# The beginning of the second attention in another issue order on four engines, and its later part left to the scheduler

## The chip, the cores and the metric

The kernel runs on one core of a Trainium2 chip. A core has five engines that work side by side, each with its own instruction stream: PE (matrix products, written to the PSUM memory), DVE (vector work), ACT (scalar functions), POOL (more vector work, masks) and SP (issues transfers). POOL issues transfers too. Engines wait for each other through semaphores. An engine takes its instructions in the order in which they were issued to it, so an instruction that waits holds up all that stands behind it on the same engine.

The metric is the device time of one execution in microseconds (us), the median over several runs.

## The reference

The reference is one layer of a decoder trunk on 1024 tokens of width 1024. One input projection feeds four groups of heads; their gated outputs are put side by side, go through one output projection, are added to the input, and are normalised at the end:

```python
def forgetting_attention(q, k, v, log_f):        # the "second attention" here: fox
    cum = jnp.cumsum(log_f, axis=-1)
    ...
        logits = (jnp.einsum('bhqd,bhkd->bhqk', qb, k) * scale
                  + cb[..., None] - cum[:, :, None, :])
        logits = jnp.where(key_pos[None, :] <= q_pos[:, None], logits, -jnp.inf)
        return jnp.einsum('bhqk,bhkd->bhqd', jax.nn.softmax(logits, axis=-1), v)
...
def reference(x, norm_g, w_in, ..., w_out, final_g):
        h = rms_norm(x, norm_g[l])
        p = h @ w_in[l]
        y_fox = forgetting_attention(...)
        y_sb = stick_breaking_attention(...)     # the first attention here: sb
        y_rw = rwkv7_time_mix(...)
        y_lru = rg_lru(...)
        y = jnp.concatenate([
            y_fox * jax.nn.silu(fg.astype(f32)),
            y_sb * jax.nn.silu(sg.astype(f32)),
            y_rw * jax.nn.silu(rg.astype(f32)),
            y_lru * jax.nn.silu(lg.astype(f32)),
        ], axis=-1).astype(x.dtype)
        x = x + y @ w_out[l]
    return rms_norm(x, final_g)
```

## The kernel before

Most products are made of two or three products of rounded parts (a high and a low part of each factor), so that nearly every tile has a twin: `woh` and `wol` are the high and low parts of a block of the output weights, `PH` and `PL` those of transposed attention weights.

The kernel's last third, from about 400 us on, is what the change touches. There the first attention (sb) ends, the second (fox) runs, and PE has "fill" beside both. The fill beside sb is the input projections (`pj_fv`: the values of fox, the last of them). The fill beside fox is the output projection `po` (768 of its 1024 input rows: groups sb, RWKV, LRU), eight blocks of 128 tokens by two halves of columns. The remaining 256 input rows, those of fox itself, are `pofx` at the end, and the final norm follows.

Attention works in units: a pair of heads (0 or 1), a group g of 256 queries, a head o of the pair. In `fox_weights` a unit makes scores on PE (`zfox`, L1174, in one of two PSUM banks "g"), adds the forget term to them and takes the maximum on DVE (`atfox`, L1213; `Fb` is the forget row spread over all partitions, `FM` a masked piece of it that POOL makes at L1197), takes the exponential on ACT (L1222), a reciprocal on DVE (`sm`, L1226), and scales on ACT (L1229). In `values` PE transposes the weights (`ptfox`, L1246, in one of two PSUM banks "c"), ACT and DVE copy them out as `PH` and `PL` (L1251, L1252), and PE multiplies them with the values `VS` (`avfox`, L1256). ACT and DVE add the two halves up (`ypfox`, L1260 and L1261), DVE multiplies with the gate `gt` (L1145), and the result is written to memory (`yx_d`, L1391) through `yyfox`. The sb attention goes through the same `values` (`ptsb`, `PHsb`, `PLsb`, `avsb`). Digits in a name are pair-head, query block or group, and part: `PLsb331` is head 3, group 3, part 1; `zfox050` is head 0, query block 5, part 0.

The transfers around it: SP's queue brings keys (`KSfox`, L1117, four loads of 256 KB for a pair), the forget rows (`Fb`, L1129, 512 KB each), queries (`Q`, L1108, 64 KB), values (`VS`, L1124), gates (`gt`, L1132, 512 KB); POOL's queue stores the projected values (`p_fv`, L1006), and loads the output projection's left factors (`yc`, L1403, two loads of 768 KB for 256 tokens), the residual (`xt`, L1409, 256 KB) and raw output weights (`wor`, L1331). A block `po` is closed by DVE's addition `ac` (L1353), which needs `xt`.

The order of each engine's instructions is written out as numbers. `ORDERS` (from L55) has a text for each engine; `in_order()` (L1474) chains the instructions named there, one behind the other, without a wait between them; instructions that are not named are placed by the framework's list scheduler. `order()` (L1263) chains PE's fill between the attention's products in any case.

Of the kernel before, what the change touches and what calls it, by code (L numbers as in the profile page):

```python
# [42 lines left out]
for _name, _w in (  # L43
# [163 lines left out]
    ),  # L207
}
# [1342 lines left out]
```

## Time and profile before

| | us |
|---|---|
| runs before: lowest, median, highest | 625.92, 629.45, 630.3 |
| the profiled execution's own time | 629.03 |
| its span, first to last instruction | 627.1 |
| PE busy in the span | 608.5 (97%) |
| DVE busy | 489.8 (78%) |
| ACT busy | 390.7 (62%) |
| POOL busy | 200.8 (32%) |

The time lies 1.93 us above the span. Busy time says how much of the span an engine had an instruction under way; with PE at 97% it is PE's few idle stretches, and those in which its clock is low, that can be won or lost. The views used are: the table of windows (busy time of each engine in a stretch of time, the number of its instructions in brackets, then the granted clock of PE, the busy share of the transfer engines, and GB/s); the list of waits (an engine and line, who released it, total, number of times, longest); and the timeline (start, duration, engine, line, operation, result and operands, the number of merged instructions, and in brackets the idle time before it and who ended that). In the timeline neighbouring instructions overlap a little, since each row's duration runs to the end of its pipeline.

### The profile page before, as it was taken

How to read it: one execution, taken by the hardware profiler on the slowest of the kernel's cores; microseconds unless marked ns; L12 is line 12 of the kernel's file. 1: busy time of each engine (PE TensorE's matmuls, PEld its weight loads, DVE VectorE, ACT ScalarE, POOL GpSimd, SP SyncE). 2: the span in 40 equal slices, each digit the busy share in tenths (PEclk: the TensorE clock that was granted, in tenths of full speed). 3: DMA queues.
4: the chain of work that ended last, by engine and by line, in shares of the span. 5: the costliest groups of instructions: out<-in, count | busy, mean ns of one | idle time of the engine just before them, and what ended most of it. 6: DMA issues, size and time to landing. Idle time of an engine off the chain costs nothing.

```text
span 627.1 us, 11831 instructions
## 1 busy us (share of the span) xinstructions
PE 608.5 (97%) x4060; PEld 494.9 (79%) x4060; DVE 489.8 (78%) x1131; ACT 390.7 (62%) x722; POOL 200.8 (32%) x328
## 2 busy tenths in 40 slices
PE   8999999999999999999999999999999999999993
PEld 6867777778876687777888888879997788888882
DVE  6598687998996796978866988888774776857687
ACT  6797948451013378797534776567764657766575
POOL 2231421313113675444343220400223222322175
PEclk9999999999999999999999999999999899999997
DMA  8873766527351336721998665355498867763225
GB/s 288 305 220 87 193 176 152 143 101 183 108 165 62 103 99 222 241 100 71 254 300 270 202 211 159 134 169 168 143 273 298 261 207 248 256 197 135 84 102 201
DMA packets 86403, 114.35 MB, mean 182 GB/s; under 512 B 38151, under 2 KB 57927, under 8 KB 86344
## 3 DMA queue, kind: packets, MB, share of 16 engines
q1 hardware_dynamic: 69112, 57.81, 31.0%
q0 software_dynamic: 16656, 55.23, 26.1%
q8 instruction: 32, 0.52, 0.3%
q10 hardware_dynamic: 576, 0.56, 0.3%
q14 instruction: 27, 0.22, 0.1%
HBM read 79.31 MB, written 33.21 MB: 179 GB/s over the span
## 4 chain that ended last, share of the span: by engine, by line
PE 65%; DVE 13%; ACT 7%; DMA 7%; issue 6%; POOL 2%; SPq 1%; DVEq 0%; ACTq 0%; POOLq 0%
PE po L1351 9%; PE pj_fk L402 4%; PE pofx L1351 4%; PE pj_sg L402 4%; PE pj_fq L402 3%; PE pj_sq L402 3%; PE pj_rg L402 3%; PE pj_fg L402 3%; PE zsb L1174 3%; PE avfox L1256 3%; PE pj_v L402 3%; PE zfox L1174 2%; PE avsb L1256 2%; PE ptfox L1246 2%; DMA xr<-in_xT_dram 2%
## 5 line engine op out<-in xcount | busy, mean ns | idle before, releaser
L1351 PE MATMUL po<-woh,yc 128*128 128x512 f32 x192 | 69.6, 412 | 0.0
L1190 DVE TENSOR_TENSOR_SCAN atsb<-kp,atsb 128x128 f32<-128x128 f32 (+7 forms) x32 | 43.4, 1362 | 5.1 <-ACT atsb L1188 4.9
L1351 PE MATMUL po<-wol,yc 128*128 128x512 f32 x96 | 39.8, 414 | 0.0
L1222 ACT ACTIVATE atfox<-atfox,nb 128x128 f32<-128x128 f32 (+7 forms) x32 | 24.6, 770 | 23.9 <-DVE nb L1219 12.7
L1351 PEld LDWEIGHTS po<-woh,yc 128*128 128x128 f32 x192 | 34.8, 192 | 2.9
L1187 ACT ACTIVATE kp<-zsb 128x512 f32<-128x512 f32 (+3 forms) x48 | 23.6, 491 | 17.5 <-PE zsb L1174 17.0
L1252 DVE TENSOR_TENSOR PLfox<-ptfox,PHfox 128x512 fp32r<-128x512 f32 (+1 forms) x40 | 25.4, 636 | 10.4 <-ACT PHfox L1251 9.8
L1252 DVE TENSOR_TENSOR PLsb<-ptsb,PHsb 128x512 fp32r<-128x512 f32 (+1 forms) x40 | 25.1, 630 | 8.3 <-ACT PHsb L1251 7.5
L1251 ACT ACTIVATE PHsb<-ptsb 128x512 fp32r<-128x512 f32 (+1 forms) x40 | 22.1, 555 | 10.8 <-PE avsb L1256 5.9
L1251 ACT ACTIVATE PHfox<-ptfox 128x512 fp32r<-128x512 f32 (+1 forms) x40 | 21.9, 548 | 11.1 <-PE avfox L1256 9.7
L1174 PE MATMUL zsb<-KSsb,Q 128*128 128x512 f32 (+3 forms) x96 | 28.6, 357 | 0.0
L1174 PE MATMUL zfox<-KSfox,Q 128*128 128x512 f32 (+3 forms) x96 | 25.6, 349 | 2.2 <-DVE mx L1213 2.2
L1229 ACT ACTIVATE atfox<-atfox,sm 128x128 f32<-128x128 f32 (+7 forms) x32 | 23.4, 767 | 0.7 <-DVE sm L1226 0.7
L1188 ACT ACTIVATE atsb<-zsb 128x512 f32<-128x512 f32 (+3 forms) x48 | 23.4, 488 | 0.0
L749 POOL TENSOR_TENSOR Hp<-UV,PC 64x128 f32<-64x128 f32 x32 | 16.6, 518 | 21.3 <-DVE UV L796 17.6
L1174 PEld LDWEIGHTS zfox<-KSfox,Q 128*128 128x128 f32 x96 | 17.8, 191 | 6.2 <-DVE mx L1213 2.6
L1246 PE MATMUL ptsb<-ident,atsb 128*128 128x128 f32 x144 | 22.2, 272 | 0.4 <-DVE PLsb L1252 0.4
L1381 POOL TENSOR_TENSOR ac<-ac,fg 128x512 f32<-128x512 f32 x16 | 20.7, 1324 | 5.6 <-ACT ot L1359 5.6
L1213 DVE CUSTOM_DVE_ANT_0 atfox<-zfox,Fb 128x512 f32<-128x512 f32 (+3 forms) x40 | 20.9, 524 | 2.0 <-PE zfox L1174 1.8
L1246 PEld LDWEIGHTS ptfox<-ident,atfox 128*128 128x128 f32 x144 | 18.2, 140 | 5.5
L1246 PE MATMUL ptfox<-ident,atfox 128*128 128x128 f32 x144 | 22.2, 272 | 0.0
L1256 PE MATMUL avsb<-PLsb,VS 128*128 128x256 f32 x80 | 20.1, 286 | 0.9 <-DVE PLsb L1252 0.7
(547 smaller groups left out, 2161.6 us busy)
## 6 DMA issues: line engine op xcount, KB each, us to landing
yc<-yx_d POOLq DMA_DIRECT2D x16, 768.0 KB, 6.9
xn<-in_x_dram SPq DMA_DIRECT2D x8, 512.0 KB, 5.3
Q<-p_sq SPq DMA_DIRECT2D x64, 64.0 KB, 3.4
Q<-p_fq SPq DMA_DIRECT2D x64, 64.0 KB, 3.6
xt<-in_x_dram POOLq DMA_DIRECT2D x16, 256.0 KB, 6.1
out_dram<-ac SPq DMA_DIRECT2D x15, 256.0 KB, 2.1
xr<-in_xT_dram SPq DMA_DIRECT2D x6, 512.0 KB, 9.0
wor<-in_w_out_dram SPq DMA_DIRECT2D x9, 256.0 KB, 3.8
```

What stands on the lines that cost most here:

```text
L402: mm = nc.tensor.matmul(out[0:ww.shape[-1]], ww, xx[hf][:, k], start=(k == 0 and xx is xh and ww is wh), stop=(k == KT - 1 and ww is wl))
L1174: ((hi - c) / 2400, nc.tensor.matmul(z[:, c - lo:hi - lo], q, k, start=j == 0, stop=j == len(ops) - 1))
L1187: nc.scalar.activation(kp[:, lo:hi], z[:, 0:hi - lo], AF.Sigmoid, scale=-0.125)
L1188: nc.scalar.activation(at[:, lo:hi], z[:, 0:hi - lo], AF.Sigmoid, scale=0.125)
L1190: nc.vector.tensor_tensor_scan(rv, kp[:, 0:n][:, ::-1], rv, 0.0, op0=ALU.mult, op1=ALU.add)
L1222: exp = nc.scalar.activation(At[qb][:, 0:n], At[qb][:, 0:n], AF.Exp, bias=nb[:, qb:qb + 1], scale=0.125, accum_out=sm_[:, 0, qb:qb + 1])
L1229: nc.scalar.activation(At[qb][:, 0:n], At[qb][:, 0:n], AF.Copy, scale=sm_[:, 1, qb:qb + 1])
L1246: T.append((P / 1200, nc.tensor.transpose(pt[:, col:col + P], At[qb][:, (2 * m + j) * P:(2 * m + j + 1) * P], ident)))
L1251: nc.scalar.activation(PH[:, 0:w], pt[:, 0:w], AF.Copy)
L1252: nc.vector.tensor_tensor(PL[:, 0:w], pt[:, 0:w], PH[:, 0:w], op=ALU.subtract)
L1256: V.append(((c1 - c0) / 2400, nc.tensor.matmul(av[:, q0:256], VS[:, 2 * m + j, :], pp[:, c0:c1], start=m == 0 and j == 0 and pi == 0, stop ...
L1351: mm = nc.tensor.matmul(po, y, w, start=i == 0, stop=i == len(ops) - 1)
```

## The change

Only `ORDERS` changes. In the text of DVE, ACT, POOL and SP some numbers from the beginning of fox on stand in another order, and behind that beginning all five texts are cut off: what follows is placed by the scheduler. The table is 34 lines shorter, so that a line number of the old kernel is 34 higher than the new one's for the same statement. Two of the changed lines, SP's:

```diff
-        "266 207 242-245 267 260 275 246-249 276 223 284 268-271 261 277 262 278-280 232 286-289 274 290-293 313 "
-        "283 314 322 241 323 295 272 296-301 281 302 331 250 304 273 282 305-311 285 315-318 324-327 294 336 337 "
...
+        "266 207 242-245 267 260 275 246-249 276 223 284 268-271 261 277 262 278-280 232 286-289 274 290 293 292 "
+        "291 314 313 322 283 323 295-298 241 299 272 281 302 300 301 304 305 307 306 331 308 311 309 310 250 273 "
+        "282 315-318 285 324-327 294"
```

The built programs have the same instructions. PE's order is the same in both, row for row, also behind the place where its text ends. On the other engines rows move at several places. Three are shown; a row has the line, the operation, result and operands with their buffer numbers, and the size.

First, SP's queue where fox's keys of pair 0 (`KSfox1` is the second such tile) and the forget row `Fb1` are loaded. Before:

```order
L1108 DMA Q_4411<-p_fq_2265 64x256 x4
L1117 DMA KSfox1_6559<-p_fk_2418 64x1024
L1129 DMA Fb1_5960<-F_d_129 128x1024
L1117 DMA KSfox1_6559<-p_fk_2418 64x1024 x2
L1391 DMA yx_d_128<-yysb12_5291 128x2x256
L1117 DMA KSfox1_6559<-p_fk_2418 64x1024
L1108 DMA Q_4411<-p_fq_2265 64x256
L1124 DMA VS_4410<-p_fv_2720 128x4x128
L1108 DMA Q_4411<-p_fq_2265 64x256 x6
L1124 DMA VS_4410<-p_fv_2720 128x4x128
```

The same place of SP's queue now:

```order
L1083 DMA KSfox1_6559<-p_fk_2418 64x1024 x3
L1095 DMA Fb1_5960<-F_d_129 128x1024
L1083 DMA KSfox1_6559<-p_fk_2418 64x1024
L1074 DMA Q_4411<-p_fq_2265 64x256 x4
L1357 DMA yx_d_128<-yysb12_5291 128x2x256
L1074 DMA Q_4411<-p_fq_2265 64x256
L1090 DMA VS_4410<-p_fv_2720 128x4x128 x2
```

Two loads of keys now stand ahead of `Fb1` that stood behind it, and the first load of values stands behind four more rows, with the second right behind it.

Second, DVE at the same time of the program, where the last unit of sb (`PLsb33..`) overlaps the first of fox. Before:

```order
L1342 TENSOR_TENSOR wol21_5630<-wor21_5494,woh21_5629 128x512
L1252 TENSOR_TENSOR PLsb330_5421<-ptsb330_5415,PHsb330_5420 128x512
L1252 TENSOR_TENSOR PLsb331_5434<-ptsb331_5428,PHsb331_5433 128x512
L1226 RECIPROCAL sm_00_5970<-sm_00_5970 128x2
L1213 ISA atfox10_6012,mx10_6009<-zfox100_6013,FM10_6005 128x128
```

DVE's same place now:

```order
L1218 TENSOR_TENSOR PLsb330_5421<-ptsb330_5415,PHsb330_5420 128x512
L1116 TENSOR_TENSOR yysb12_5291<-ypsb12_5143,yysb12_5291 128x256
L1179 ISA atfox10_6012,mx10_6009<-zfox100_6013,FM10_6005 128x128
L1179 ISA mx10_6009 128x1
L1308 TENSOR_TENSOR wol21_5630<-wor21_5494,woh21_5629 128x512
L1218 TENSOR_TENSOR PLsb331_5434<-ptsb331_5428,PHsb331_5433 128x512
L1192 RECIPROCAL sm_00_5970<-sm_00_5970 128x2
```

`atfox10`, which needs `FM10` and through it `Fb1`, has moved ahead of `PLsb331`; `wol21` has come between them.

Third, DVE some 20 us later, where the first block of the output projection is closed (`ac0`). Before:

```order
L1353 TENSOR_TENSOR ac0_5527<-po00_5540,xt00_5538 128x512
L1218 TENSOR_REDUCE nb11_6134<-mx11_6119 128x2
L1219 TENSOR_SCALAR nb11_6134<-nb11_6134 128x2
L1201 MEMSET mx12_6263 128x6
L1226 RECIPROCAL sm_11_6121<-sm_11_6121 128x2
L1213 ISA atfox04_6187,mx02_6184<-zfox040_6188,Fb0_5950 128x512
```

DVE's same place now:

```order
L1179 ISA atfox04_6187,mx02_6184<-zfox040_6188,Fb0_5950 128x512
L1179 ISA mx02_6184 128x1
L1192 RECIPROCAL sm_11_6121<-sm_11_6121 128x2
L1111 TENSOR_TENSOR ypfox00_5963<-ypfox00_5963,gt_4412 128x256
L1179 ISA atfox04_6187,mx02_6184<-zfox041_6192,FM02_6180 128x128
L1179 ISA mx02_6184 128x1
L1319 TENSOR_TENSOR ac0_5527<-po00_5540,xt00_5538 128x512
L1218 TENSOR_TENSOR PLfox010_6090<-ptfox010_6084,PHfox010_6089 128x512
```

`atfox04<-zfox040` no longer stands behind `ac0` and the reciprocal. On POOL the load of `xt00` has moved from behind the two loads `yc10` to ahead of them. The gate's product `ypsb13*gt`, behind which SP loads the next gate, has moved on DVE from ahead of `atfox12` to behind it.

Later, where ACT rounds the last blocks of output weights, three of these have moved ahead of the copies of one unit. Before:

```order
L1251 ACTIVATE PHfox132_6504<-ptfox132_6499 128x512
L1260 ACTIVATE ypfox03_6339<-avfox03_6379 64x256
L1251 ACTIVATE PHfox133_6516<-ptfox133_6512 128x384
L1341 ACTIVATE woh71_5655<-wor71_5653 128x512
L1341 ACTIVATE woh00_6533<-wor00_6531 128x512
L1260 ACTIVATE ypfox03_6339<-avfox13_6472 64x256
L1341 ACTIVATE woh10_6539<-wor10_6537 128x512
```

ACT's same place now:

```order
L1307 ACTIVATE woh71_5655<-wor71_5653 128x512
L1217 ACTIVATE PHfox132_6504<-ptfox132_6499 128x512
L1307 ACTIVATE woh00_6533<-wor00_6531 128x512
L1307 ACTIVATE woh10_6539<-wor10_6537 128x512
L1217 ACTIVATE PHfox133_6516<-ptfox133_6512 128x384
```

On DVE `wol71`, `wol00` and `wol10` have moved in the same way against `PLfox132`, `PLfox133` and `atfox37`. In the final norm ACT scales `ac2` and takes a root ahead of the squares `ot10`, `ot11`, where one of the two scalings stood between them.

55 rows, old and new, of the table ORDERS are left out of this document.

## The prediction

> **What bounds the kernel now.** I read the page's head and its busy times first, then the windows of 5 us, to find where PE is not busy, then the timeline there. A window's columns are PE, PE's weight loads, DVE, ACT and POOL busy, PE's granted clock, the share of the transfer engines, GB/s.
>
> ```profile
> span 627.1 us, 11831 instructions
> PE 608.5 (97%) x4060; PEld 494.9 (79%) x4060; DVE 489.8 (78%) x1131; ACT 390.7 (62%) x722; POOL 200.8 (32%) x328
> ...
> 460.00:465.00 5.00, 4.64 (x40) 4.40 (x39) 4.08 (x13) 4.20 (x9) 0.00 (x0) 1.00 1.03 301
> 485.00:490.00 5.00, 2.91 (x9) 2.55 (x10) 3.63 (x11) 4.00 (x10) 1.33 (x3) 0.69 0.73 226
> 490.00:495.00 5.00, 5.00 (x29) 4.19 (x28) 3.61 (x15) 3.12 (x7) 1.69 (x3) 0.96 0.87 271
> 530.00:535.00 5.00, 5.00 (x30) 4.26 (x30) 3.77 (x11) 5.00 (x9) 0.77 (x2) 1.00 0.55 163
> ```
>
> PE is busy 97% of the span. In the window from 530 it is busy all the time at clock 1.00; idle PE time shows between 460 and 465 (0.36 us) and from 485 to 490 (2.1 us), and only with the second is the granted clock low (0.69, then 0.96). So a wait costs time here only where it reaches PE, and then one for one, plus what the clock loses behind it.
>
> **The stall that the change removes.** The rows of PE, DVE, ACT and POOL around 485:
>
> ```profile
> 484.49 0.40 PE L1351 MATMUL po<-wol,yc 128*128 128x512 f32 x1
> 487.09 1.22 PE L1174 MATMUL zfox<-KSfox,Q 128*128 128x512 f32 x2 [2.20 <-DVE mx L1213]
> 490.53 0.40 PE L1174 MATMUL zfox<-KSfox,Q 128*128 128x256 f32 x2
> ...
> 483.83 0.69 DVE L1353 TENSOR_TENSOR ac<-po,xt 128x512 f32<-128x512 f32 x1 [3.16 <-DMA xt<-in_x_dram]
> 486.27 0.17 DVE L1226 RECIPROCAL sm<-sm 128x2 f32<-128x2 f32 x1 [1.47 <-ACT atfox L1222]
> 486.35 0.67 DVE L1213 CUSTOM_DVE_ANT_0 atfox<-zfox,Fb 128x512 f32<-128x512 f32 x1
> ...
> 471.66 1.70 POOL L1403 DMA_DIRECT2D yc<-yx_d  x2 [1.20 <-PE zfox L1174]
> 473.34 0.56 POOL L1409 DMA_DIRECT2D xt<-in_x_dram  x1
> ```
>
> At 487.09 `zfox050` needs a bank that `atfox04<-zfox040` (486.35) frees. That stood on DVE behind `ac0`, which waited 3.16 us for `xt00` (issued at 473.34, behind 1.5 MB of `yc10`), and behind the reciprocal, which waited another 1.47 us for ACT. Now `atfox04<-zfox040` stands ahead of both, and `xt00` is issued ahead of `yc10`. PE's 2.20 us go. How much the clock lost behind them follows from the work up to 490.53: six products of 512 columns and four of 256. At full clock they follow each other as here:
>
> ```profile
> 473.96 0.39 PE L1351 MATMUL po<-wol,yc 128*128 128x512 f32 x1
> 474.19 0.62 PE L1351 MATMUL po<-woh,yc 128*128 128x512 f32 x2
> 474.65 0.27 PE L1256 MATMUL avfox<-PHfox,VS 128*128 128x256 f32 x1
> 474.77 0.28 PE L1256 MATMUL avfox<-PLfox,VS 128*128 128x256 f32 x1
> ```
>
> 0.23 us apart for 512 columns, 0.12 for 256: 6 x 0.23 + 4 x 0.12 = 1.86 us, against 490.53 - 487.09 = 3.44 measured. So 1.6 us went to the clock. Removed: 2.2 + 1.6 = 3.8 us. The ends: 0 if the wait only changes its name (below), 3.8 if nothing comes in its place.
>
> The Trainium skill's page "TensorE: Matmul & The Clock Gate" (section "Why this matters for your kernels") says that PE falls back to half clock after an idle gap of more than about 3 us. This trace disagrees: 2.20 us of idle were enough for 0.69. By the page only 2.2 us would go here, while a new gap of 3 us would cost its 1.6 us of half clock as well; the sum below would then be 631.8 instead of 630.2. I go by the trace for both.
>
> **The stall that the change brings.** Where sb ends, DVE, POOL, PE and SP did this, and the transfers of `KSfox` took (view of one tile, issue to landing):
>
> ```profile
> 466.92 0.29 DVE L1213 CUSTOM_DVE_ANT_0 atfox<-zfox,FM 128x128 f32<-128x128 f32 x1 [1.50 <-POOL FM L1197]
> 467.14 0.69 DVE L1342 TENSOR_TENSOR wol<-wor,woh 128x512 fp32r<-128x512 f32 x1
> 467.74 0.69 DVE L1252 TENSOR_TENSOR PLsb<-ptsb,PHsb 128x512 fp32r<-128x512 f32 x1
> 466.49 0.76 POOL L1197 TENSOR_SCALAR_AFFINE_SELECT FM<-Fb 128x256 f32<-128x256 f32 x2 [9.18 <-DMA Fb<-F_d]
> ...
> 464.81 0.66 PE L1246 MATMUL ptsb<-ident,atsb 128*128 128x128 f32 x4 [0.36 <-DVE PLsb L1252]
> 466.71 0.49 PE L1246 MATMUL ptsb<-ident,atsb 128*128 128x128 f32 x3
> ...
> 453.54 0.33 SPq L1129 DMA_DIRECT2D Fb<-F_d  x1
> 453.97 1.36 SPq L1117 DMA_DIRECT2D KSfox<-p_fk  x2
> DMA to landing us min/median/max: 12.2/12.8/13.5
> ```
>
> Before, DVE's 1.50 us of waiting for `FM10` harmed nobody: `PLsb331`, which frees the bank of `ptsb333` (PE, 466.71), stood ahead of it. Now `PLsb331` stands behind `atfox10` and `wol21`. `Fb1` landed at 466.49. The two loads of keys that now go ahead of it were issued at 453.97 and some 0.68 later (half of 1.36), and with 12.2 to 13.5 us to landing the later of them was there at 466.9 to 468.2. `Fb1` is now the last of that same set of bytes, issued at about the same time, so it lands 0.4 to 1.7 us later; I take 0.9, nearer to the small end because the set is all that has to pass: 467.4. Then `FM10` and the way to DVE 0.43 (466.92 - 466.49), `atfox10` 0.22 (467.14 - 466.92), `wol21` 0.60 (467.74 - 467.14) and `PLsb331` 0.69: 469.3. PE is at `ptsb333` at 466.71 - 0.36 = 466.35, since the 0.36 us at 464.81 goes: ACT's `PHsb330` has moved ahead of a table load and an exponential, so `PLsb330` comes earlier. The new stall is 469.3 - 466.35 = 3.0 us (2.1 if `Fb1` lands as before, 3.8 at the other end). It is longer than the 2.20 us that lowered the clock, so I add the same 1.6 us (0 at the other end: the 0.36 us left the clock of its window at 1.00). Together +4.6, less 0.36.
>
> The Trainium skill's page "DMA: Bandwidth & Descriptors" (section "Queues, rings and completion order") says that descriptors of one queue are taken in ring order, and gives 435 GB/s as the ceiling of the fabric; 512 KB more ahead would be an estimated 1.2 us by this page instead of 0.9, a sum of 630.5. The trace can't separate the queue's own order from POOL's loads beside it.
>
> **Smaller terms.** *The gate and the values.* Rows of DVE, SP, PE, and the landing times of `VS`:
>
> ```profile
> 475.91 0.34 SPq L1132 DMA_DIRECT2D gt<-p_fg  x1
> 478.03 0.29 DVE L1213 CUSTOM_DVE_ANT_0 atfox<-zfox,FM 128x128 f32<-128x128 f32 x1
> 487.52 0.42 DVE L1145 TENSOR_TENSOR ypfox<-ypfox,gt 128x256 f32<-128x256 f32 x1
> 466.64 0.38 SPq L1124 DMA_DIRECT2D VS<-p_fv  x1
> 467.52 0.39 PE L1174 MATMUL zfox<-KSfox,Q 128*128 128x256 f32 x2
> DMA to landing us min/median/max: 2.7/4.2/6.7
> ```
>
> `ypsb13*gt` now comes behind `atfox12`, whose last piece is the row at 478.03, so SP loads the next gate at about 478.7 of the old clock instead of 475.91. Its product, `ypfox00*gt`, now stands on DVE ahead of `PLfox010`, for which PE asks four products of 512 columns behind `zfox050`: at 484.9 + 4 x 0.23 + 0.1 = 485.9, without the stall. From the gate's arrival to there DVE does 0.42 for the product, some 0.3 for `atfox04`'s masked piece, `ac0` and `PLfox010` at 0.69 each: 2.1 us. So `gt` has 485.9 - 2.1 - 478.7 = 5.1 us to land. A load of `VS` took up to 6.7 (1.6 late) or 4.2 (hidden), one of the crowded keys 12.8 (7.7 late). I take 0.7, half of the first, as `VS` is the neighbour in time; the ends are 0 and 7.7. The first `VS` itself is now issued behind queries that wait for `zfox110` (467.52 + 0.39 = 467.9) where it went out at 466.64. It has 474.65 - 467.9 = 6.7 us until `avfox00`, just its longest landing time: 0.
>
> *The output weights at 530 to 541.*
>
> ```profile
> 532.68 2.07 ACT L1229 ACTIVATE atfox<-atfox,sm 128x896 f32<-128x896 f32 x2
> 534.66 0.62 ACT L1341 ACTIVATE woh<-wor 128x512 fp32r<-128x512 f32 x1
> 536.30 0.54 POOL L1331 DMA_DIRECT2D wor<-in_w_out_dram  x1 [0.99 <-DVE wol L1342]
> 537.55 0.56 DVE L1252 TENSOR_TENSOR PLfox<-ptfox,PHfox 128x384 fp32r<-128x384 f32 x1 [0.34 <-ACT PHfox L1251]
> 539.40 0.29 PE L1256 MATMUL avfox<-PLfox,VS 128*128 128x256 f32 x1
> DMA to landing us min/median/max: 2.8/2.9/8.3
> ```
>
> `PHfox133` now stands behind `woh71`, `woh00` and `woh10`, but `woh61` (534.66) has moved ahead of the two scalings (2.07 us), so the raw block `wor10`, which its partner `wol61` lets go, is issued some 2 us earlier: 536.30 - 2 + 2.9 to land (the last row, for `wor`) = 537.2. Then `woh10` 0.62, `PHfox133` about 0.5, a turn on DVE behind `wol00`, 0.2, and `PLfox133` 0.56: 539.1. PE wants it at 539.40. Cover of 0.3 us is thin; I take 0.3 of loss, between 0 and 5.4 - 0.3 = 5.1 (a landing of 8.3 instead of 2.9).
>
> *The end.* POOL waited 1.08 us for the square of the last block's second half; ACT now does both halves in a row:
>
> ```profile
> 619.08 2.66 POOL L1381 TENSOR_TENSOR ac<-ac,fg 128x512 f32<-128x512 f32 x2 [1.08 <-ACT ot L1359]
> ```
>
> One of the two products can start up to 1.08 us earlier, but the row scale that the block needs hangs on the second square; I take -0.3, between -1.08 and +0.7 (one more scaling on ACT ahead of the squares, at the 0.62 of ACT's 512 columns). All else that moves I put at 0: PE's order is unchanged, and PE's full windows are the cover; where that is thin the cost is a wait on PE like the 0.36 us above.
>
> **The sum.** From the profiled execution's 629.03 (span 627.1 and 1.93 around it; 0.42 below the median 629.45, so the two can be used alike): -3.8 - 0.36 + 4.6 + 0.7 + 0.3 - 0.3 = +1.1, that is 630.2. The change trades one stall for another.
>
> **Rivals.**
> *A, faster.* The old stall goes and the new one is short: `Fb1` lands as before, 2.1 us, the clock holds, the gate and the weights cost nothing. 629.03 - 3.8 - 0.36 + 2.1 - 0.3 = 626.7. For it: `Fb1` and the keys are issued together, and 0.36 us of idle left the clock alone. Against: 2.20 us did not.
> *B, slower.* The first `VS` is late. It is needed 6.7 us after its issue, its own longest landing, but the keys in the same queue took 13.5. From 6.7 us on PE stalls at `avfox00`, one for one, and the clock's 1.6 us come on top: landing at 10 gives 630.2 + 3.3 + 1.6 = 635.1, at 11 it gives 636.1. It is slower than before in any case, and by over 1% from 10.6 us on.
> *C, no change in time.* The rows that moved find cover, or the new stall takes back just what the old one gave: 629.0. PE's unchanged order speaks for it; `PLsb331` behind `wol21` speaks against it.
> *D, the clock.* The low clock from 485 on did not need the gap of 2.20 us, and stays, while a longer gap earns its own: 630.2 + 1.6 = 631.8. The windows speak against it: clock 1.00 where PE was never idle. By the Trainium skill's rule on gaps above ("TensorE: Matmul & The Clock Gate") this is the time that comes out.
>
> **Chances.** My forecast 0.45 (own range 628.3 to 632.7: the new stall at 2.1 or 3.8, the gate at 0 or 1.6, the weights at 0 or 1.2), A 0.2, B 0.12, C 0.18, D 0.05. The time is that of the likeliest, 630.2. The range takes in A and B up to 11 us: 626 to 636. About 1%, 6.3 us, is what a measurement of this kernel can tell from no change. Faster by that needs 623.2, which none of the cases gives: 0.05 for what is not on the list. Slower by that needs 635.7, most of B or the long ends of gate and weights: 0.13. The same: 0.82.
>
> **What would show it.** In the changed kernel's profile: PE idle about 3 us at `ptsb` near 466, released by DVE `PLsb`, with a granted clock below 0.9 in the window behind; POOL's wait for `Fb` ending near 467.4 rather than 466.5; no idle PE at `zfox` near 487, and DVE not waiting for `xt`; DVE waiting for `gt` at L1111 or not at all; no wait of PE over 0.5 us at `avfox` near 540. It is wrong if `Fb1` lands before 466, if PE waits for `VS`, or if PE's idle time sits in a place not named here.

## The result and the profile after

| | us |
|---|---|
| before, 19 runs: lowest, median, highest | 624.55, 626.74, 634.52 |
| changed, 19 runs: lowest, median, highest | 627.82, 631.05, 635.17 |
| ratio of the two | 1.0061, 95% interval 1.0044 to 1.0079 |
| profiled execution, changed: own time and span | 632.37, 630.6 |
| profiled execution, before: own time and span | 629.03, 627.1 |

Ratios and their intervals here are estimated from the single runs, a slow one (634.52) left out, and can differ by some 0.1% from the quotient of the medians shown.

The changed kernel is 0.6% slower, 3.8 us (2.8 to 5.0). The forecast was +1.1 us on 629.03. That the time, 631.05, is near the forecast 630.2 is in part luck, since two errors cancel: before's median over 19 runs is 2.3 us below the execution from which the sum was made, and the rise is more than three times what was predicted.

The head of the changed kernel's page, and PE's waits in it from 455 us on (who waited, at which line, for whom: total, times, longest):

```profile
span 630.6 us, 11832 instructions
PE 609.0 (97%) x4060; PEld 495.8 (79%) x4060; DVE 489.7 (78%) x1131; ACT 391.2 (62%) x722; POOL 200.6 (32%) x328
```

```profile
PE ptsb L1212 <- DVE sm L1192: 5.2, 1, 5.2
PE avfox L1222 <- DVE PLfox L1218: 0.4, 1, 0.4
PE pofx L1317 <- DVE ac L1319: 0.3, 1, 0.3
```

PE was as busy as before (609.0 against 608.5), and the span grew by 3.5 us. One long wait is left: `ptsb`, where the forecast had it, but 5.2 us instead of 3.0. The windows of the changed kernel, with the same columns as in the prediction:

```profile
460.00:465.00 5.00, 5.00 (x45) 5.00 (x45) 2.41 (x11) 4.20 (x9) 0.00 (x0) 1.00 1.02 304
465.00:470.00 5.00, 0.76 (x7) 0.56 (x5) 0.67 (x3) 0.60 (x1) 1.10 (x3) 1.00 0.45 123
470.00:475.00 5.00, 4.02 (x19) 4.05 (x20) 2.92 (x9) 1.50 (x4) 1.74 (x4) 0.51 0.53 182
475.00:480.00 5.00, 5.00 (x32) 4.73 (x31) 2.55 (x14) 2.56 (x9) 2.44 (x5) 0.80 0.81 242
485.00:490.00 5.00, 5.00 (x28) 4.22 (x28) 3.81 (x15) 4.04 (x11) 0.41 (x1) 1.00 1.04 351
540.00:545.00 5.00, 4.59 (x26) 3.70 (x25) 4.94 (x14) 2.25 (x5) 3.72 (x6) 1.00 0.74 220
```

The 0.36 us of idle PE time between 460 and 465 and the 2.1 us from 485 to 490 are gone. From 465 to 470 every engine is nearly idle, and then PE's clock is 0.51 and 0.80. How the idle stretch came about, in the timeline of SP, POOL, DVE and PE, in the landing times of `Fb`, and in two windows of 1 us:

```profile
451.27 2.25 SPq L1083 DMA_DIRECT2D KSfox<-p_fk  x3
453.61 0.54 SPq L1095 DMA_DIRECT2D Fb<-F_d  x1
...
468.90 0.76 POOL L1163 TENSOR_SCALAR_AFFINE_SELECT FM<-Fb 128x256 f32<-128x256 f32 x2 [12.15 <-DMA Fb<-F_d]
...
469.33 0.29 DVE L1179 CUSTOM_DVE_ANT_0 atfox<-zfox,FM 128x128 f32<-128x128 f32 x1 [6.06 <-POOL FM L1163]
469.55 0.69 DVE L1308 TENSOR_TENSOR wol<-wor,woh 128x512 fp32r<-128x512 f32 x1
470.15 0.68 DVE L1218 TENSOR_TENSOR PLsb<-ptsb,PHsb 128x512 fp32r<-128x512 f32 x1
470.75 0.15 DVE L1192 RECIPROCAL sm<-sm 128x2 f32<-128x2 f32 x1
...
470.98 0.87 PE L1212 MATMUL ptsb<-ident,atsb 128*128 128x128 f32 x3 [5.22 <-DVE sm L1192]
...
476.77 0.37 PE L955 MATMUL pj_fv<-wl_fv,xh 128*128 128x256 f32 x1
476.98 0.28 PE L955 MATMUL pj_fv<-wh_fv,xh 128*128 128x256 f32 x1
...
DMA to landing us min/median/max: 4.0/9.6/15.2
...
467.00:468.00 1.00, 0.00 (x0) 0.00 (x0) 0.00 (x0) 0.00 (x0) 0.00 (x0) 1.00 0.20 50
468.00:469.00 1.00, 0.00 (x0) 0.00 (x0) 0.00 (x0) 0.00 (x0) 0.10 (x1) 1.00 0.11 41
```

`Fb1` is issued at 453.61, practically when it was before (453.54), and POOL's wait for it ends at 468.90: 15.3 us, where it was 12.95 (453.54 to 466.49). In the last two microseconds of this wait hardly anything moved: 50 and 41 GB/s, with the transfer engines busy at 0.20 and 0.11. DVE waits 6.06 us for the mask, then does `atfox10`, `wol21` and `PLsb331`, and only then PE goes on. The wait names the reciprocal (L1192), the last row on DVE before PE started; that PE did not need the reciprocal, and went on as soon as `PLsb331` was done, is shown by the first experiment. Behind the wait products of 256 columns follow each other 0.21 us apart up to 476.98 (the last step is 476.98 - 476.77) and not 0.12 as before: some 6.0 us (476.98 - 470.98) at half clock, of which 3.0 are lost.

### The profile page after: what moved, and what is told of

It is laid out like the page before. It is cut to its first block, busy times and chain, and to the rows that moved or that the text cites. A ratio compares the mean times of both kernels' runs of the same rounds, so it can differ in the third digit from the quotient of the medians.

```text
span 630.6 us, 11832 instructions
## 1 busy us (share of the span) xinstructions
PE 609.0 (97%) x4060; PEld 495.8 (79%) x4060; DVE 489.7 (78%) x1131; ACT 391.2 (62%) x722; POOL 200.6 (32%) x328
## 4 chain that ended last, share of the span: by engine, by line
PE 74%; DVE 9%; ACT 6%; issue 6%; POOL 2%; DMA 2%; SPq 0%; DVEq 0%; POOLq 0%; ACTq 0%
PE po L1317 8%; PE pj_fk L368 4%; PE pj_r L368 4%; PE pj_lg L368 4%; PE pj_rg L368 3%; PE pj_sg L368 3%; PE pj_lx L368 3%; PE pj_v L368 3%; PE pj_fq L368 3%; PE pj_sq L368 3%; PE pj_fg L368 3%; PE zsb L1140 3%; PE pj_k L368 3%; PE pj_fv L955 3%; PE avsb L1222 3%
## 5 line engine op out<-in xcount | busy, mean ns | idle before, releaser
L1212 PEld LDWEIGHTS ptsb<-ident,atsb 128*128 128x128 f32 x144 | 17.8, 141 | 8.6 <-issue 5.4
L1163 POOL TENSOR_SCALAR_AFFINE_SELECT FM<-Fb 128x256 f32<-128x256 f32 x16 | 7.0, 440 | 53.1 <-DVE mx L1179 26.3
```

What stands on the lines that cost most here:

```text
L1212: T.append((P / 1200, nc.tensor.transpose(pt[:, col:col + P], At[qb][:, (2 * m + j) * P:(2 * m + j + 1) * P], ident)))
```

## The experiments

Two parts of the change met at `ptsb`: DVE's order (`PLsb331` behind `atfox10`) and SP's order (three key loads ahead of `Fb1`, not one). Three kernels undo these one by one and together, and a fourth undoes both and writes the later part out again; one takes the half step, one does DVE's part alone in the kernel before, and two attack the old stall from its two sides. The times are compared with runs of the kernel before on the same chip.

### e1_plsb_first: DVE's part undone

The numbers are DVE's rows: 728 is `PLsb331`, 772 and 768 are `atfox10` and the reciprocal, 744 is `wol21`.

```diff
-        "772 744 728 768 745 729 773 313 314 730 774-776 793 783 784 777 315 316 731 769 785-788 806 770 794 795 "
+        "728 772 744 768 745 729 773 313 314 730 774-776 793 783 784 777 315 316 731 769 785-788 806 770 794 795 "
```

> The changed kernel with one row moved back on DVE: PLsb331 goes ahead of atfox10, all else stays. Theory (the new stall is DVE's order: PLsb331 stood behind atfox10, which waits for FM10 and so for Fb1): PE no longer idles at ptsb333 (5.22 us before), the clock of 0.51 and 0.80 behind it goes back to 1.00, together about 8 us, so about 623 us against the changed kernel's 631, some 0.6% below the kernel before. Rival (the late Fb1 alone is what hurts, whatever stands behind it on DVE): Fb1 still lands near 469, so another wait for atfox10 or the bank it frees takes the place, over 3 us of idle PE remain within 10 us, and the time is above 627.

Measured: 629.1 against 627.66, ratio 1.0035 (1.0013 to 1.0057). PE's longest wait from 455 us on, and rows of its timeline (DVE, PE, POOL):

```profile
PE avsb L1222 <- DVE PLsb L1218: 3.3, 1, 3.3
```

```profile
466.28 0.69 DVE L1218 TENSOR_TENSOR PLsb<-ptsb,PHsb 128x512 fp32r<-128x512 f32 x1 [1.26 <-ACT PHsb L1217]
471.20 0.29 DVE L1179 CUSTOM_DVE_ANT_0 atfox<-zfox,FM 128x128 f32<-128x128 f32 x1 [4.22 <-POOL FM L1163]
472.02 0.16 DVE L1192 RECIPROCAL sm<-sm 128x2 f32<-128x2 f32 x1
472.68 0.68 DVE L1218 TENSOR_TENSOR PLsb<-ptsb,PHsb 128x512 fp32r<-128x512 f32 x1
...
467.35 0.49 PE L1212 MATMUL ptsb<-ident,atsb 128*128 128x128 f32 x3
473.42 0.38 PE L1222 MATMUL avsb<-PLsb,VS 128*128 128x256 f32 x1 [3.35 <-DVE PLsb L1218]
...
470.77 0.76 POOL L1163 TENSOR_SCALAR_AFFINE_SELECT FM<-Fb 128x256 f32<-128x256 f32 x2 [12.29 <-DMA Fb<-F_d]
```

With `PLsb331` done at 466.97, `ptsb333` runs at 467.35 without a wait, long before the reciprocal (472.02): the reciprocal was not what PE waited for. But the theory that the stall hung on `PLsb331` alone, and that the time would be about 623, missed; the rival came out. `Fb1` is as late as in the changed kernel (15.2 us after its issue, 470.77 - 455.59), DVE still waits 4.22 us for the mask, and now `PLsb332`, the next row of the same unit, stands behind it; PE stalls 3.3 us at the product that needs it. Moving one row moves the stall by one tile.

The profiled execution has a second lowered stretch, not at the stall but at the kernel's start: behind 1.98 us of idle PE time at 5 us, the clock is 0.74 from 5 to 10 us and 0.92 from 10 to 15.

### e2_forget_first: SP's part undone

SP's rows 314, 313, 322, 323 are the four key loads, 283 is `Fb1`.

```diff
-        "291 314 313 322 283 323 295-298 241 299 272 281 302 300 301 304 305 307 306 331 308 311 309 310 250 273 "
+        "291 314 283 313 322 323 295-298 241 299 272 281 302 300 301 304 305 307 306 331 308 311 309 310 250 273 "
```

> The changed kernel with SP's old order of one transfer: Fb1 ahead of two of the three key loads, DVE as changed. Theory (Fb1 pays for the 512 KB that were put ahead of it): it lands some 2 us earlier, the stall at ptsb333 falls from 5.2 to 2.5 to 3.5 us, the low clock behind it shortens too, the time falls by 3 to 4 us to about 627.5. Rival (the landing is set by all traffic of that time, the order in the queue counts little): Fb1 lands within 0.7 us of where it did, stall above 4.5, time within 1 us of 631.

Measured: 625.33 against 627.66, ratio 0.9973 (0.9954 to 0.9991). PE's wait, two windows, and the issue and the landing of `Fb1` in the timeline:

```profile
PE ptsb L1212 <- DVE sm L1192: 1.6, 1, 1.6
```

```profile
465.00:470.00 5.00, 3.38 (x30) 3.21 (x29) 3.88 (x12) 2.06 (x5) 2.65 (x6) 1.00 0.69 219
470.00:475.00 5.00, 5.00 (x32) 4.45 (x31) 3.65 (x16) 2.90 (x9) 4.00 (x7) 1.00 0.94 288
```

```profile
452.68 0.33 SPq L1095 DMA_DIRECT2D Fb<-F_d  x1
...
465.01 0.76 POOL L1163 TENSOR_SCALAR_AFFINE_SELECT FM<-Fb 128x256 f32<-128x256 f32 x2 [8.56 <-DMA Fb<-F_d]
```

Two key loads fewer ahead of `Fb1`, and it lands 12.3 us after its issue instead of 15.3. The stall falls from 5.2 to 1.6 us, further than the 2.5 to 3.5 that were expected, and the clock stays at 1.00: moving two transfers turned 0.6% slower into 0.3% faster. The remaining 1.6 us are DVE's part of the change.

### e6_two_keys: the half step

```diff
-        "291 314 313 322 283 323 295-298 241 299 272 281 302 300 301 304 305 307 306 331 308 311 309 310 250 273 "
+        "291 314 313 283 322 323 295-298 241 299 272 281 302 300 301 304 305 307 306 331 308 311 309 310 250 273 "
```

> The changed kernel with Fb1 moved ahead of one of the three key loads, so that two stand ahead of it: the step between the changed kernel (three ahead, Fb1 lands 15.3 us after its issue, PE idle 5.2) and e2 (one ahead, PE idle 1.6 and the clock at 1.00). Theory (bytes ahead in the queue set the landing, about 1.8 us for each 256 KB): Fb1 lands in between, near 467, PE idles 3 to 4 us, and as that is over 2.2 us the clock falls behind it; the time is 628 to 629. Rival (only the third load matters, as it is the one that waits behind Fb0's landing): as e2, about 625.5, or as the changed kernel, about 631.

Measured: 629.83 against 628.66, ratio 1.0028 (0.9998 to 1.0059). The wait at `ptsb` is 2.3 us. The window behind it, and rows of SP, POOL and PE:

```profile
470.00:475.00 5.00, 5.00 (x32) 5.00 (x31) 2.61 (x11) 1.61 (x6) 2.00 (x4) 0.66 0.79 230
```

```profile
454.34 0.54 SPq L1095 DMA_DIRECT2D Fb<-F_d  x1
467.34 0.76 POOL L1163 TENSOR_SCALAR_AFFINE_SELECT FM<-Fb 128x256 f32<-128x256 f32 x2 [9.22 <-DMA Fb<-F_d]
...
469.42 0.52 PE L1212 MATMUL ptsb<-ident,atsb 128*128 128x128 f32 x3 [2.28 <-DVE sm L1192]
469.89 0.28 PE L955 MATMUL pj_fv<-wh_fv,xl 128*128 128x256 f32 x1
470.16 0.41 PE L955 MATMUL pj_fv<-wh_fv,xh 128*128 128x256 f32 x1
```

13.0 us to landing, between the other two, so the number of key loads ahead orders the landing times of these three (12.3, 13.0, 15.3), though not in equal steps, and the stall is shorter than the 3 to 4 us that were expected. The times also vary without a change of order: with one load ahead, from issue to the end of POOL's wait, they are 12.95 in the kernel before, 12.8 in e3, 12.2 in e4, 10.8 in e5, 11.6 in e7 and 9.8 in e8. So two loads ahead cannot be told from one; three, with 15.3 in the changed kernel and 15.2 in e1, stand apart. With 0.7 us of stall more than in e2 the clock comes down to 0.66. It does not fall where the idle time ends: the product at 469.89 still takes 0.28 us, the one at 470.16 takes 0.41.

### e3_plsb_behind: DVE's part alone, in the kernel before

```diff
-        "725 714 307 308 726 720 721 715 309 310 716 763 717 737 738 722 764 723 765 766 311 312 767 739 724 782 "
-        "744 727 728 768 772 745 729 313 314 773-776 793 730 777 731 783 784 315 316 769 785-788 732 806 789 733 "
+        "725 714 307 308 726 720 721 715 309 310 716 763 717 737 738 722 764 723 765 766 311 312 767 739 724 782 727 772 744 728 768 745 729 313 314 773-776 793 730 777 731 783 784 315 316 769 785-788 732 806 789 733 "
```

> The kernel before with DVE's rows at one place in the changed order: atfox10 and wol21 ahead of PLsb331; SP, ACT, POOL as before. Theory (DVE's order alone makes the stall; Fb1 lands as before): a stall at ptsb333 of 2 to 3 us with a low clock behind it, and the old stall near 487 still there as PE's later work is put off with its transfers: 3 to 5 us slower than before, about 631. Rival (without the late Fb1 the order costs nothing): PE idles below 0.5 us there and the time is within 1 us of before.

Measured: 626.91 against 627.66, ratio 0.9994 (0.997 to 1.0018): no difference that can be told. PE's longest wait, and two windows:

```profile
PE ptsb L1246 <- DVE sm L1226: 1.5, 1, 1.5
```

```profile
465.00:470.00 5.00, 3.12 (x26) 2.73 (x25) 2.86 (x7) 1.62 (x6) 1.83 (x4) 1.00 0.77 266
485.00:490.00 5.00, 4.58 (x26) 3.34 (x25) 3.39 (x13) 4.19 (x10) 1.33 (x2) 1.00 0.87 271
```

DVE's order alone makes a stall of 1.5 us, much the same as the 1.6 of e2, and no low clock. Expected were 2 to 3 us of stall and a time of about 631, so that missed. The old stall of 2.2 us at `zfox`, whose rows this edit does not touch, is gone too: PE is idle for 0.42 us from 485 to 490 (5.00 - 4.58), in other waits. DVE's wait for `xt`, in the timeline row of `ac0`, is shorter:

```profile
484.71 0.69 DVE L1353 TENSOR_TENSOR ac<-po,xt 128x512 f32<-128x512 f32 x1 [1.04 <-DMA xt<-in_x_dram]
```

1.04 us instead of 3.16. Counted from the issue of the load of `xt00`, DVE came to `ac0` at the same moment, 7.3 us behind it (484.71 - 1.04 - 476.33, and 483.83 - 3.16 - 473.34 in the kernel before). The load itself was quicker: 8.4 us (484.71 - 476.33) and not 10.5 (483.83 - 473.34). What made it quicker is not shown. So the old stall is not a fixed sum, and the stalls of a profile cannot simply be added up.

### e7_both: both parts undone

The two edits of e1 and e2 in one kernel.

```diff
-        "772 744 728 768 745 729 773 313 314 730 774-776 793 783 784 777 315 316 731 769 785-788 806 770 794 795 "
+        "728 772 744 768 745 729 773 313 314 730 774-776 793 783 784 777 315 316 731 769 785-788 806 770 794 795 "
...
-        "291 314 313 322 283 323 295-298 241 299 272 281 302 300 301 304 305 307 306 331 308 311 309 310 250 273 "
+        "291 314 283 313 322 323 295-298 241 299 272 281 302 300 301 304 305 307 306 331 308 311 309 310 250 273 "
```

> The changed kernel with both mendings: Fb1 ahead of two of the three key loads (e2) and PLsb331 ahead of atfox10 (e1). Theory (the new stall was order on DVE times the late Fb1; without either nothing is left): no idle PE over 0.5 us between 460 and 500, 1.6 us less than e2: 623 to 624.5, that is 0.5% below the kernel before. Rival (PLsb332, which still stands behind atfox10, waits in its place as in e1, where PE idled 3.3 us at avsb): PE idles 1 us or more at avsb and the time is as e2, 625.3.

Measured: 625.59 against 628.66, ratio 0.9961 (0.9935 to 0.9987). Its windows where the stall was:

```profile
465.00:470.00 5.00, 5.00 (x46) 5.00 (x44) 3.14 (x10) 4.15 (x9) 1.29 (x4) 1.00 0.91 286
470.00:475.00 5.00, 5.00 (x42) 4.83 (x41) 3.76 (x18) 3.17 (x10) 3.45 (x6) 1.00 0.86 264
```

PE is never idle here and the clock is 1.00. Expected were 623 to 624.5 and no idle stretch over 0.5 us there; the second came true. So the two reorderings that meet at `ptsb` account for the whole loss; the rest of the change gains.

### e8_both_old_end: e7 with the later part written out again

The changed kernel cuts the five texts off behind fox's beginning. Here before's later part is put back behind e7's texts. SP's, for example:

```diff
-        "282 315-318 285 324-327 294"
...
+        "282 315-318 285 324-327 294 336-337 321 338-341 330 342-343 303 319 348-351 320 328 352-355 329 312 360-367
...
```

> e7 with the later part of all five texts put back as in the kernel before (from where the change cuts them off), so the scheduler places nothing there. Theory (what the scheduler places costs about half a microsecond: 0.41 us at avfox near 542 and 0.3 at pofx in the changed kernel): 0.3 to 1 us faster than e7. Rival (the later part counts nothing, or the scheduler's order is better): within 0.3 us of e7, or slower.

Measured: 624.87 against 628.66, ratio 0.9942 (0.9917 to 0.9966), the best of all; it beats both kernels. PE's wait of 0.4 us at `avfox`, which e7 has as the changed kernel has it, is not in the list. Expected were 0.3 to 1 us less than e7. The median is 0.7 us lower, but the two intervals overlap, so the later part's worth is not settled.

### e4_ac0_behind and e5_xt00_first: the old stall, from two sides

Both start from the kernel before. e4 puts `ac0` (740) and the reciprocal (800) behind `atfox04<-zfox040` (807) on DVE; e5 puts the load of `xt00` (259) ahead of the two loads `yc10` (262, 261) on POOL.

```diff
-        "794 795 770 778 796 797 740 798 799 819 800 807 779 780 790 808 781 791 809 741 810-813 834 792 820 814 "
+        "794 795 770 778 796 797 798 799 819 807 740 800 779 780 790 808 781 791 809 741 810-813 834 792 820 814 "
```

> The kernel before with only DVE's ac0 and the reciprocal sm_11 behind atfox04<-zfox040; xt00 is still loaded behind yc10. Theory (the old stall was DVE's queue: atfox04 waited behind ac0, not for its own data): the 2.20 us at zfox050 and the low clock behind them go, 3 to 4 us, about 623. Rival (the late xt00 is the cause and the wait only moves to the next row behind ac0): PE idles over 1 us at ptfox or avfox behind it, and the time is within 1.5 us of before.

```diff
-        "173-175 258 257 176 293 177 295 297 178 265 266 179 299 262 261 259 180 260 301 303 263 269 268 264 305 "
+        "173-175 258 257 176 293 177 295 297 178 265 266 179 299 259 262 261 180 260 301 303 263 269 268 264 305 "
```

> The kernel before with only POOL's load of xt00 ahead of the two loads yc10; DVE's order as it was. Theory (the old stall is DVE's queue: atfox04<-zfox040 stands behind ac0 and behind the reciprocal, which both wait): with xt00 landing early ac0 no longer waits, so the reciprocal's own wait of about 1.5 us on ACT is what is left, and PE idles under 0.5 us at zfox050: the same gain as moving DVE's rows, about 0.4% (2 to 3 us). Rival (the yc10 loads pushed back by xt00 are missed by the next block po20): PE waits for yc and nothing is gained.

Measured: e4 624.83 against 627.66, ratio 0.9968 (0.995 to 0.9986); e5 627.31 against 628.66, ratio 0.9985 (0.9952 to 1.0019), not told from no change. The windows of e4, and of e4's timeline the rows of DVE:

```profile
480.00:485.00 5.00, 5.00 (x29) 4.18 (x29) 3.46 (x14) 3.14 (x8) 0.96 (x2) 1.00 0.78 296
485.00:490.00 5.00, 5.00 (x30) 4.26 (x29) 4.67 (x18) 2.57 (x7) 2.65 (x4) 1.00 0.93 305
```

```profile
481.62 0.69 DVE L1213 CUSTOM_DVE_ANT_0 atfox<-zfox,Fb 128x512 f32<-128x512 f32 x1 [0.62 <-PE zfox L1174]
482.86 0.69 DVE L1353 TENSOR_TENSOR ac<-po,xt 128x512 f32<-128x512 f32 x1 [0.54 <-DMA xt<-in_x_dram]
```

In both profiles the stall at `zfox` is gone. In e4 the transfer takes 9.7 us, not much less than the 10.5 of the kernel before; the row that waits for it stands where its wait harms nobody. That is the change's mechanism for the old stall, and nothing came in its place. But it is worth 2.0 us (0.9 to 3.1) by e4, not the 3 to 4 that were expected. For e5 a gain of 2 to 3 us was expected: its interval neither shows nor excludes it.

## Why the prediction was partly right

**What the change removes.** Right in mechanism: no idle PE time at `zfox`, and no wait of DVE for `xt`. Too large in size: 2.2 us of idle and 1.6 of clock were taken as what every execution pays. Each run's mean granted clock says otherwise. The profiled run of before has 0.992. Of the 66 runs of the same kernel that were made beside the experiments 16 were at 0.993 or below (median 629.8 us) and 50 at 0.994 or above (627.6). The ten profiled executions say what such a mean stands for: 0.994 to 0.996 in the six with no lowered stretch ahead of PE's last product, 0.992 and 0.991 in the two with one (before, e6), 0.989 and 0.988 in the two with twice that (changed, e1). So the clock falls somewhere in about one execution of four, most often, it seems, behind the old stall, and the profiled one was of these. The median execution has at most the 2.2 us alone, and the 2.0 that e4 measures fits that. The prediction set the profiled execution 0.42 us below the median of three; by 19 runs it lies 2.3 above.

**What the change brings.** Right in place, chain and sign: `Fb1`, the mask, `atfox10`, `wol21`, `PLsb331`, PE at `ptsb333`; e2, e1 and e7 show that both orders are needed for the 5.2 us. The term that was mis-sized is `Fb1`'s landing: "I take 0.9, nearer to the small end because the set is all that has to pass", with 1.7 as the far end. From issue to landing it became 2.3 us more (15.3 - 12.95). The reasoning took the four keys and `Fb1` as one set that ends when it did; but in before a key load that lay behind `Fb1` could end later and harm nobody, and `Fb1`'s own place in it is what counts. That the set ended later here is not explained by the bytes alone: from 467 to 469 the transfer engines were nearly idle (0.20 and 0.11), as in e1 from 469 to 471 (0.49 and 0.18), while the last full microsecond ahead of `Fb1` had 0.71 in the kernel before and 0.74 in e2. What holds the last part of the load up is open. The rest of the stall's excess is PE, which came to `ptsb333` at 465.76 (470.98 - 5.22) and not at 466.35: it was ahead, and ahead only means waiting longer.

By the Trainium skill's page "DMA: Bandwidth & Descriptors" (section "Queues, rings and completion order") descriptors of one queue are taken in ring order on each transfer engine; the landing times agree in so far as three loads ahead make `Fb1` later than one. The page's ceiling of 435 GB/s gave an estimate of 1.2 us for the 512 KB; the runs show 2.3. In the window from 460 the transfer engines were busy all the time (1.02) at 304 GB/s, some of it for POOL's queue (its store `p_fv`, issued at 456.17, landed 10.3 us later). Sharing can account for a part of the difference only, since the engines were nearly idle in the last two microseconds.

**The clock behind the new stall.** Predicted 1.6 us from the row of 2.20 us, 3.0 in the profile: a longer idle stretch does not cost the same clock once but about twice (6.0 us at half speed against 3.4; the last section says why). It too varies: of the 19 changed runs 9 were at 0.989 or below like the profiled one (median 633.2 us), 7 at 0.992 or 0.993 (629.6), and 3 above (628.1).

**The sum, redone.** Each row takes the waits of its own profile: less 2.2 for the old stall, less 0.36 where that wait went too, plus the new stall, plus 1.7 us for each lowered stretch (0.34 of 5 us, from e6's window) times the share of runs that have it, less 0.4 for before's one in four. A run at 0.991 to 0.993 counts as one stretch, one at 0.990 or below as two, wherever in the kernel they lie. Waits of 0.2 to 0.6 us at `avfox` and `pofx`, which most of these kernels have, are left out. The sum was worked out after the runs, and with these runs' own clocks, so it is a check of consistency, not a forecast.

| kernel | new stall, us | runs with a lowered stretch | sum, us | measured, us (95%) |
|---|---|---|---|---|
| changed | 5.2 | 16 of 19, 9 of them two | +4.5 | +3.8 (2.8 to 5.0) |
| e1 | 3.3 | 7 of 10, 2 of them two | +1.9 | +2.2 (0.8 to 3.6) |
| e6 | 2.3 | 6 of 10 | +0.3 | +1.8 (-0.1 to 3.7) |
| e3 | 1.5 | 1 of 10 | -0.9 | -0.4 (-1.9 to 1.1) |
| e2 | 1.6 | 1 of 10 | -1.2 | -1.7 (-2.9 to -0.6) |
| e4 | 0 | 0 of 10 | -2.6 | -2.0 (-3.1 to -0.9) |
| e5 | 0 | 1 of 10, that one two | -2.3 | -0.9 (-3.0 to 1.2) |
| e7 | 0 | 1 of 12 | -2.8 | -2.5 (-4.1 to -0.8) |
| e8 | 0 | 1 of 12 | -2.8 | -3.6 (-5.2 to -2.1) |

Every sum lies in its interval. e6's stands nearest to the edge of one.

**The smaller terms.** The gate: predicted +0.7, it cost nothing, and the prediction had the wrong load. In the changed kernel the load of `gt` was issued at 484.45 and landed 5.8 us later, at 490.25, but `ypfox00*gt` had already run at 488.82 without a wait. The kernel keeps one half of `gt` for each pair of heads: that product reads pair 0's, which was loaded at 423.1 and landed 5.6 us later, and the load at 484.45 is pair 1's, needed only behind 544.71, where pair 0's last product stands. So this term had nothing to wait for. The values: 0 as predicted; up to 500 us `VS` landed in 4.8 us at most. The output weights: predicted +0.3, and PE has 0.4 at `avfox` near 540 (5.00 - 4.59 in its window), at the product of `PLfox133`. The size and the place fit; the path does only in part, since ACT's one wait for raw weights there, 0.56 us, stood ahead of `woh71` and not of `woh10`. The end: predicted -0.3, measured 0, since the last 10.0 us behind PE's last product are as long as before. `pofx` waits 0.3 us, which it did not before; the prediction did not name that place.

**The rivals.** A fell, since `Fb1` did not land as before and the clock did not hold; e2 is about what A described, with other means. B fell: no wait of PE for `VS`. C fell: the interval excludes 1, although 0.6% is less than the 1% that the prediction took for the least that can be told. D fell as written, since the clock was low only behind a gap.

## What to carry to other kernels

When rows of an in-order engine are reordered, price the new row at the head not by its own work but by the latest thing it waits for, and follow what stands behind it to the engine that is the bound; here a DVE row that waited for a transfer took PE with it, and moving one row away moved the stall to the next one. Price a moved transfer by its own place in the queue, not by when the set of transfers ends, and leave room for its spread: in the four kernels with before's SP order the same load took 10.8 to 12.95 us. Before a sum is made from a profiled execution, see whether it is a typical one: the mean granted clock of each run told two groups of runs apart, which a median of three could not.

## What the runs showed of the hardware

PE's granted clock changed at fixed intervals of 3.413 us, wherever in them an idle stretch began. Windows of 0.5 us place each change, since the clock was either 1.00 or 0.50: a window at 0.94 had 0.44 us at 1.00 and 0.06 at 0.50. The first two rows are of the kernel before, the others of the changed one:

```profile
486.50:487.00 0.50, 0.00 (x0) 0.00 (x0) 0.50 (x2) 0.47 (x2) 0.00 (x0) 0.94 1.21 345
490.00:490.50 0.50, 0.50 (x3) 0.39 (x2) 0.50 (x3) 0.00 (x0) 0.50 (x1) 0.65 0.41 115
...
470.00:470.50 0.50, 0.00 (x0) 0.00 (x0) 0.50 (x2) 0.00 (x0) 0.18 (x1) 0.63 0.05 18
476.50:477.00 0.50, 0.50 (x5) 0.50 (x4) 0.02 (x2) 0.45 (x3) 0.37 (x1) 0.54 0.86 253
623.50:624.00 0.50, 0.00 (x0) 0.00 (x0) 0.47 (x3) 0.00 (x0) 0.50 (x2) 0.73 0.00 0
```

In the kernel before the clock falls at 486.94 and rises at 490.35, 3.41 us later. In the changed kernel it falls at 470.13, while PE still stands idle, rises at 476.96, two intervals later (6.83), and falls again behind PE's last product at 623.73: 153.6 us behind the first fall, 45 times 3.413. Worked out in the same way, the falls in the kernel before (486.94 and 620.06) are 39.0 intervals apart, those in e6 (470.08 and 620.27) 44.0, those in e1 (7.37, 474.99 and 621.77) 137.0 and 43.0.

What decided a fall was how much of the interval that ended there PE had been idle. Over all whole intervals of the ten profiles, laid out from the falls, the clock, when at 1.00, fell behind every one with 1.84 us of idle time or more (the least is e1's from 471.58 to 474.99) and behind none with 1.71 or less (the most is e3's from 615.37 to 618.79). So the position of a stall counts beside its length. The 2.2 us of the kernel before had 2.06 in one interval; the 1.6 us of e2 were too short to lower the clock anywhere; the 5.2 us took in a whole interval, and the clock stayed low for two: the first of them began with 0.85 us of idle time.

Runs with a mean clock of 0.993 or below were 1 of 10 each at 1.5 and 1.6 us of idle, 16 of 66 at 2.2, 6 of 10 at 2.3, 7 of 10 at 3.3 and 16 of 19 at 5.2. The four kernels without a long stall (e4, e5, e7 and e8) had it in 3 of 44 runs, so that other places can lower the clock too, as the start did in e1. These shares are not odds by length: each length is that of the one profiled execution, and how long the stall was in the other runs is not on record.

The Trainium skill's page "TensorE: Matmul & The Clock Gate" (section "Why this matters for your kernels") gives a gap of about 3 us as the limit. The runs put it lower: 2.28 us of idle were followed by 0.66 in e6, 2.20 by 0.69 in the kernel before, and 1.84 us within one interval were enough in e1.
